# Powers in another tile, the finish over more heads, a later norm and an earlier start of sums in a two-block network

## The chip, the cores and the metric

The kernel runs on one core of a Trainium2 chip. The metric is the device time of one execution in microseconds; lower is better. Times come from the device, the rows from one execution that was taken with the hardware profiler.

## What is computed

Two blocks follow each other on one sequence of 1024 tokens with 1024 channels, in float32. The first block has two layers, each with a mixer and a feed-forward layer; the second block has an mLSTM branch, a state-space (S5) branch and gates.

```python
def first_block(x, ...):
    for layer in range(2):
        h = rmsnorm(x, mix_pre_g[layer])
        m = even_mixer(h, ...) if layer % 2 == 0 else odd_mixer(h, ...)
        x = x + rmsnorm(m, mix_post_g[layer])
        h = rmsnorm(x, ffn_pre_g[layer])
        x = x + rmsnorm(swiglu(h, w_gate, w_up, w_down), ffn_post_g[layer])
    return x

def second_block(h, ...):
    xn = rmsnorm_2(h, norm_pre_g)
    u_a, z_a, o_a, i_a, f_a, u_b, z_b, g_pre = split(xn @ w_in)
    y_a = mlstm_branch(u_a, z_a, o_a, i_a, f_a, ...) @ w_a_out
    y_b = s5_branch(u_b, z_b, lam_re, lam_im, log_dt, B, C, ...) @ w_b_out
    g = sigmoid(g_pre)
    return h + rmsnorm_2((g[..., :D] * y_a + g[..., D:] * y_b) @ w_o, norm_post_g)
```

The state-space branch needs, for each of its 16 groups of states, a table of 256 rotations exp(i n angle). It is built by doubling from the powers exp(i 2^k angle), k = 0 to 7.

## The kernel before, in words

**Tiles.** Activations lie with channels on the 128 partitions, as eight tiles of 128 channels by 512 tokens for each half of the sequence (half 0 and half 1). Every float32 product is made of three matmuls on a high and a low part of each operand. So each weight tile and each activation tile is first split: ScalarE writes the high part (L186 for weights, L246 for activations), VectorE or GpSimd subtracts it for the low part (L188, L248, L250).

**Buffers.** Tiles with one tag share a fixed number of buffers: 27 of tag `t4` (128 x 2 x 512), 18 of tag `t2` (128 x 512), one of `junk` (128 x 512 in bfloat16, 1024 bytes on a partition). Buffers are handed out when the program is built, in a planned order of the work. At run time an instruction that writes a buffer waits for the last readers of what was in it before. All loads and most stores are issued by SyncE's queue (SP) in that planned order, one behind the other.

**Side work.** Generators do work beside the main loop over matmuls. `start(g, rate)` enters one, each `tick` of the main loop advances it by `rate` steps, `drain(g)` runs what is left at once. The order in the program is the priority for the planner; each engine then executes its own list in order.

**First feed-forward layer, second product.** `ffn` multiplies in `ffn_down` (L632 to L634) by the down weights for half 0, then for half 1. Each takes 22 tiles of the hidden layer (`hid`, tag `t4`), which `hid_steps` loads from DRAM (`hidd`) into `t2` buffers called `xt` (L260) and splits (L246, L250). The 22 tiles of half 1 take the buffers of those of half 0. Beside the products of the first layer run `s5_tables` (rate 2.6): small operations of VectorE on tiles of 128 x 16, and from L1318 on GpSimd's loop over the pairs of groups. In each of its 8 rounds GpSimd builds two tables in the tile `s5R` with 48 multiplies, adds and subtracts and issues their two stores (L1335). The powers that it reads, `E`, are slices of the two `t2` tiles called `s5c`, which also hold the other constants and are stored to DRAM once (L1338).

**After it.** `finish_steps` for half 1 (the norm of the product, the sum with the residual, the statistics of the sum: 13 steps) runs beside the next mixer, `odd_mixer`, at one step a tick. That mixer goes over four heads for half 0, then for half 1; a head is `odd_conv` (PSUM tile `pxr`), `odd_gate` (`pg`) and `odd_rec` (`pr`, `pi`), two ticks each. At head 1, after its gate, `finished()` runs what is left of the finish, and `norm_steps` of half 1 starts: it makes the eight normed and split tiles `xs` that half 1's first `odd_conv` reads.

**Second block, late units.** `block2` ends its mLSTM branch beside five calls of `late_firsts`, each with two units of 24 matmuls (PSUM tile `pl`) on half 0's input, c = 28, 32, 36, 40, 44. Beside them `sum_steps` loads the kept input (`kept`) and makes from it the 19 sums and split tiles that `late_rest` reads next (20 steps, five for each of four groups of tiles).

Of the kernel before, what the change touches and what calls it, by code (L numbers as in the profile page):

```python
# [11 lines left out]
F32 = mybir.dt.float32  # L12
# [9 lines left out]
NT = 8  # L22
# [27 lines left out]
class Weights:  # L50
# [13 lines left out]
    def part(self, k0):  # L64
        return Weights(self.parts, self.q, self.k0 + k0)


class Model:
# [571 lines left out]
    def ffn(self, l, B, keep, pre, hook, beside, F, done=0):  # L640


        self.ahead = 90
        n = FFT // 2
        for j in range(n - F + done, n):
            if j == n - F + done + 3:
                self.finished()
                nb = self.start(self.ffn_sums(*pre, B, keep), 5.2 / (F - done - 3))
            self.ffn_first(l, 2 * j, B, None)
        self.drain(nb)  # L650
        self.ahead = 150
        hid = [], []
        for j in range(n):
            if j == n - 1:
                nb = self.start(self.hid_steps(0, hid[0]), 3.0)
            self.ffn_quad(l, 2 * j, B, j >= n - F)
        self.flush()
        self.drain(nb)
        self.ahead = 90
        bg = self.start(*beside)  # L660
        m, ss = self.ffn_down(l, 0, hid[0])
        hid[0].clear()
        nb = self.start(self.hid_steps(1, hid[1]), 3.0)
        self.drain(nb)
        self.finish(0, m, ss, "ffn_post_g", l)
        nb = self.start(chain(self.after(self.fin), hook()), 1.0)
        m, ss = self.ffn_down(l, 1, hid[1])
        self.drain(nb)
        self.drain(bg)
        self.finish(1, m, ss, "ffn_post_g", l)  # L670

    def after(self, g):

# [561 lines left out]
    def s5_tables(self):  # L1235
# [8 lines left out]
        def sm(n):  # L1244
            i = self.s5n[n] = len(self.s5n)
            return big[i // 32][:, i % 32]
# [31 lines left out]
        V.tensor_tensor(t0, mag, mag, ALU.mult)  # L1278
        V.tensor_tensor(self.rho4, t0, t0, ALU.mult)

        E = [(sm(f"er{k}"), sm(f"ei{k}")) for k in range(8)]
        cur = (cs, sn)
        for k in range(-2, 8):
            o = E[max(k, 0)]
            if k > -2:
# [32 lines left out]
        for g0 in range(0, 16, 2):  # L1318
            G.memset(R[:, :, 0, 0:1], 1.0)
            G.memset(R[:, :, 1, 0:1], 0.0)  # L1320
            for k in range(8):
                n = 1 << k
                er, ei = (E[k][i][:, g0:g0 + 2].unsqueeze(2).to_broadcast([128, 2, n]) for i in range(2))
                s, d = slice(0, n), slice(n, 2 * n)
# [526 lines left out]
    def block2(self, xsA, norm, dst):  # L1851

        io = self.io
        xs = [xsA, []]
        self.s5_in(xs[0], 0)
        self.xs_store(xs[0], 0)
        st = self.mconv(xs[0], 0, 0)
        g = self.start(self.mgates(xs[0], 0))
        self.mout(xs[0], 0, st)
        self.finished()  # L1860
        nb = self.start(norm(xs[1]), 3.0)
        self.mz(xs[0], 0, st)
        self.drain(nb)
        self.s5_in(xs[1], 1)
        self.xs_store(xs[1], 1)
        self.drain(g)
        self.start(self.s5_main(), 2.2)
        a = b = ()
        for h in range(NH):
            for hd in range(4):  # L1870
                units = 2 * ("o" not in st) + 2 * ("z" not in st) + 2 * (hd < 3 or h == 0) + 10 * (hd == 3 and h == 1)
                self.drain(a)
                a, b = b, self.start(self.mattn(h, hd, st), self.TH / units)
                new = None
                if "o" not in st:
                    self.mout(xs[h], hd, st)
                if hd < 3:
                    new = self.mconv(xs[h], h, hd + 1)
                if "z" not in st:
                    self.mz(xs[h], hd, st)  # L1880
                if hd == 3 and h == 0:
                    xs[1] = self.xs_load(1)
                    g = self.start(self.mgates(xs[1], 1))
                    new = self.mconv(xs[1], 1, 0)
                    self.drain(g)
                st = new

        x0 = self.xs_load(0)
        B = {"b11": x0[:4], "b21": x0[4:]}
        for c in range(28, 48, 4):  # L1890
            if c == 36:
                got = self.fetch([self.kept[h][k + j] for k in range(NT // 2) for j in (0, NT // 2) for h in range(2)])
                nb = self.start(self.sum_steps(lambda k, h: next(got), NT // 2, B), 1.75)
            self.late_firsts((c, c + 2), x0)
        self.drain()
        self.ahead = 150
        pre = [[], [], []], [[], [], []]
        for c in range(28, 48, 2):
            if c == 42:
                nb = self.start(self.merge_prep(1, *pre[1], 3), 1.6)  # L1900
            self.late_rest(c, B)
        self.drain(nb)
        self.ahead = 90
        nb = self.start(self.merge_prep(1, *pre[1]), 2)
        mg = self.merge(1, nb, *pre[1])
        nb = self.start(self.merge_prep(0, *pre[0]), 2.5)
        m, ss = self.proj_out(io["w2_o"], mg)
        self.drain(nb)
        self.finish(1, m, ss, "norm_post_g_2", 0, dst=dst(1))
        mg = self.merge(0, (), *pre[0])  # L1910
        m, ss = self.proj_out(io["w2_o"], mg, last=True)
        self.finished()
        self.finish(0, m, ss, "norm_post_g_2", 0, dst=dst(0), last=True)
        self.finished()

    def run(self, out):
        io = self.io
        xs = [None, None]
        part = lambda ap: lambda h: [ap[128 * k:128 * k + 128, h * T:h * T + T] for k in range(NT)]
        self.x, self.r = [part(io["x"])(h) for h in range(NH)], [None, None]  # L1920

        B, keep = [{}, {}], [[self.dp.tile([128, T], F32, name=f"keep{l}_{k}") for k in range(NT)] for l in range(2)]
        self.hidd = [[self.dp.tile([128, T], F32, name=f"hidd{h}_{j}") for j in range(FFT)] for h in range(NH)]
        self.kept = [[self.dp.tile([128, T], F32, name=f"kept{h}_{k}") for k in range(NT)] for h in range(NH)]
        self.lated = [{c: self.dp.tile([128, T], F32, name=f"lated{h}_{c}") for c in range(28, 48)} for h in range(NH)]
        self.m1l = {c: self.dp.tile([128, T], F32, name=f"m1l{c}") for c in range(28, 48, 2)}
        self.m1d = [self.dp.tile([128, T], F32, name=f"m1d{j}") for j in range(FFT)]

        def side():

            nb = self.start(self.norm_keep(0, "ffn_pre_g", 0, B[0], keep[0]))
            self.tick(1)
            self.drain(nb)
            self.ffn_first(0, FFT - 18, B[0], None)

        def hook(gname, gi, keep=None):
            def steps():
                xs[0] = []
                yield from self.norm_steps(0, gname, gi, xs[0], keep)
            return steps  # L1940

        self.ahead = 90
        self.layer0(lambda h, *m: self.finish(h, *m, "mix_post_g", 0, rate=1 + 0.25 * h, pool=h == 1), side)
        self.ffn(0, B[0], keep[0], ("ffn_pre_g", 0), hook("mix_pre_g", 1), (self.s5_tables(), 2.6), 9, 1)

        self.ahead = 90
        y, st = [[], []], {}
        for h in range(NH):
            for hd in range(4):
                if hd or not h:  # L1950
                    self.odd_conv(xs[h], h, hd, st)
                    self.odd_gate(xs[h], hd, st)
                if h == 0 and hd == 1:
                    self.finished()
                    xs[1] = []
                    nb = self.start(self.norm_steps(1, "mix_pre_g", 1, xs[1]))
                self.odd_rec(h, hd, st, y[h])
            if h == 0:
                self.drain(nb)
                st = {}  # L1960
                self.odd_conv(xs[1], 1, 0, st)
                self.odd_gate(xs[1], 0, st)
            else:
                self.finished()
                nb = self.start(self.norm_keep(0, "ffn_pre_g", 1, B[1], keep[1]), 1.2)
            self.finish(h, *self.proj_out(io["od_out"], y[h]), "mix_post_g", 1, rate=0.5 if h == 0 else 1.25, pool=h == 1)
        self.drain(nb)
        self.ahead = 90
        self.ffn(1, B[1], keep[1], ("ffn_pre_g", 1), hook("norm_pre_g_2", 0, self.kept[0]), (self.s5_tables2(), 2.6), 9)
        self.ahead = 90  # L1970
        self.block2(xs[0], lambda o: self.norm_steps(1, "norm_pre_g_2", 0, o, self.kept[1]), part(out))
# [66 lines left out]
```

## Time and profile before

| | us |
|---|---|
| median of three runs | 3279.76 (3275.04, 3279.76, 3284.11) |
| the profiled execution | 3275.86 |
| its span in the profile | 3274.2 |
| TensorE matmul busy | 3099.3 (95%) |
| VectorE busy | 2345.7 (72%) |
| ScalarE busy | 1532.8 (47%) |
| GpSimd busy | 803.9 (25%) |

Times in the rows are microseconds from the start of the span. PE is TensorE's matmuls, PEld its weight loads, DVE is VectorE, ACT ScalarE, POOL GpSimd, SPq SyncE's queue of DMA issues. A busy share tells only that an engine had an instruction running. Where an engine sat idle, the view of waits names what released it.

### The profile page before, as it was taken

To read this page: it belongs to the slowest core of one execution; us is meant where nothing else is said; L and a number is where in the kernel's file an instruction comes from. 1 tells how busy PE (TensorE), PEld (TensorE's weight loads), DVE (VectorE), ACT (ScalarE), POOL (GpSimd) and SP (SyncE) were. 2 spreads that over 40 slices of the span, in tenths; PEclk is the share of its full clock that TensorE was granted. 3 is DMA by queue.
4 is the path that set the end of the run, shared out by engine and by line. 5 is a ranking of instruction groups with operands and counts; after the bars stand their busy time and mean duration, and the time that the engine had idled before them with its cause. 6 is when DMAs were issued, how large, how long until landed. Compare 5 with 4: busy or idle time off the path is not lost. (4 is left out here: it accounts for less than half of the span.)

```text
span 3274.2 us, 42443 instructions
## 1 busy us (share of the span) xinstructions
PE 3099.3 (95%) x14200; PEld 2526.0 (77%) x14200; DVE 2345.7 (72%) x4489; ACT 1532.8 (47%) x2842; POOL 803.9 (25%) x1002
## 2 busy tenths in 40 slices
PE   8999999999994598999999999999999999999998
PEld 5777787888883487877888887777888778778886
DVE  8768857688862359777857888786688888765664
ACT  4646644333432237676443335544455444434442
POOL 4011102555367302111236540000111100153000
PEclk9999999999997799999999999999999999999999
DMA  4443445333532434334723345576644344745562
GB/s 156 157 143 127 145 153 191 103 126 126 191 115 103 151 121 150 101 125 162 253 93 130 126 144 191 199 226 240 214 136 154 129 153 136 257 140 196 187 209 97
DMA packets 227179, 511.84 MB, mean 156 GB/s; under 512 B 28040, under 2 KB 50760, under 8 KB 226960
## 3 DMA queue, kind: packets, MB, share of 16 engines
q1 hardware_dynamic: 225680, 504.93, 46.2%
q0 software_dynamic: 1280, 4.20, 0.3%
q8 instruction: 112, 1.84, 0.2%
q14 instruction: 107, 0.88, 0.1%
HBM read 386.21 MB, written 118.59 MB: 154 GB/s over the span
## 5 line engine op out<-in xcount | busy, mean ns | idle before, releaser
L188 DVE TENSOR_TENSOR wsp<-raw,wsp 128x512 fp32r<-128x512 f32 x850 | 629.8, 747 | 350.5 <-ACT wsp L186 347.2
L186 ACT ACTIVATE wsp<-raw 128x512 fp32r<-128x512 f32 x842 | 515.7, 616 | 722.5 <-PE pd L634 201.5
L632 PE MATMUL pd<-hid,wsp 128*128 128x512 f32 x704 | 279.2, 398 | 76.6 <-ACT hid L246 76.6
L633 PE MATMUL pd<-hid,wsp 128*128 128x512 f32 x704 | 278.9, 397 | 3.5 <-DVE hid L250 3.2
L634 PE MATMUL pd<-hid,wsp 128*128 128x512 f32 x704 | 277.6, 394 | 0.0
L632 PEld LDWEIGHTS pd<-hid,wsp 128*128 128x128 f32 x704 | 133.9, 190 | 105.6 <-ACT hid L246 78.7
L495 PE MATMUL qy<-st,wsp 128*128 128x512 f32 x464 | 180.7, 389 | 3.9 <-DVE st L248 3.9
L494 PE MATMUL qy<-st,wsp 128*128 128x512 f32 x464 | 181.1, 390 | 0.2 <-ACT st L246 0.2
L496 PE MATMUL qy<-st,wsp 128*128 128x512 f32 x464 | 180.6, 389 | 0.0
L526 POOL TENSOR_TENSOR qv<-qv,qu 128x512 f32<-128x512 f32 x54 | 90.6, 1677 | 341.8 <-ACT wsp L186 226.6
L633 PEld LDWEIGHTS pd<-hid,wsp 128*128 128x128 f32 x704 | 133.9, 190 | 37.3 <-DVE hid L250 10.1
L248 POOL TENSOR_TENSOR xs<-xt,xs 128x512 fp32r<-128x512 f32 x28 | 40.8, 1457 | 483.6 <-ACT xs L246 424.8
L634 PEld LDWEIGHTS pd<-hid,wsp 128*128 128x128 f32 x704 | 134.0, 190 | 26.9
L186 ACT ACTIVATE wsp<-wss 128x512 fp32r<-128x512 f32 x108 | 68.1, 631 | 183.9 <-PE qz L496 90.3
L494 PE MATMUL pf<-xs,wsp 128*128 128x512 f32 x288 | 114.0, 396 | 9.5 <-ACT m L572 8.5
L270 DVE TENSOR_TENSOR sq<-sq 128x512 f32<-128x512 f32 x140 | 99.0, 709 | 32.1 <-ACT sq L268 31.6
L250 DVE SCALAR_TENSOR_TENSOR hid<-xt,hid 128x512 fp32r<-128x512 f32 x88 | 58.0, 689 | 84.3 <-ACT hid L246 83.6
L495 PE MATMUL pf<-xs,wsp 128*128 128x512 f32 x288 | 113.3, 394 | 0.4 <-POOL xs L248 0.4
L496 PE MATMUL pf<-xs,wsp 128*128 128x512 f32 x288 | 113.3, 394 | 0.0
L405 POOL TENSOR_TENSOR xt<-xt,m 128x512 f32<-128x512 f32 x12 | 18.2, 1524 | 364.9 <-DVE m L402 356.7
L495 PEld LDWEIGHTS qy<-st,wsp 128*128 128x128 f32 x464 | 87.1, 188 | 22.1 <-DVE st L248 4.2
L494 PEld LDWEIGHTS qy<-st,wsp 128*128 128x128 f32 x464 | 87.1, 188 | 20.3 <-DVE qu L515 1.8
(720 smaller groups left out, 9106.3 us busy)
## 6 DMA issues: line engine op xcount, KB each, us to landing
raw<-in_w_in_dram SPq DMA_DIRECT2D x86, 512.0 KB
xt<-xres SPq DMA_DIRECT2D x128, 256.0 KB
raw<-in_wd_dram SPq DMA_DIRECT2D x64, 512.0 KB
raw<-in_wg_dram SPq DMA_DIRECT2D x62, 512.0 KB
raw<-in_wu_dram SPq DMA_DIRECT2D x62, 512.0 KB
hidd<-th SPq DMA_DIRECT2D x88, 256.0 KB
xt<-hidd SPq DMA_DIRECT2D x88, 256.0 KB
raw<-in_ev_in_dram SPq DMA_DIRECT2D x32, 512.0 KB
```

The costliest lines, as they stand in the source:

```text
L186: nc.scalar.activation(sp[:, 0], raw, AF.Copy)
L188: nc.vector.tensor_tensor(sp[:, 1], raw, f(sp[:, 0]), ALU.subtract)
L248: (low or nc.vector).tensor_tensor(t[:, 1], src, f(t[:, 0]), ALU.subtract)
L250: nc.vector.scalar_tensor_tensor(t[:, 1], src, scale, f(t[:, 0]), ALU.mult, ALU.subtract)
L270: nc.vector.tensor_tensor(q, q, acc, ALU.add)
L494: nc.tensor.matmul(ps, h, xs[k][:, 0], start=start and k == 0, stop=False, skip_group_check=not start)
L495: nc.tensor.matmul(ps, h, xs[k][:, 1], start=False, stop=False, skip_group_check=not start)
L496: nc.tensor.matmul(ps, l, xs[k][:, 0], start=False, stop=k == n - 1, skip_group_check=not start)
L526: nc.gpsimd.tensor_tensor(v5, v5, u3, ALU.add)
L632: nc.tensor.matmul(ps, h_, x[:, 0], start=k0 + k == 0, stop=False)
L633: nc.tensor.matmul(ps, h_, x[:, 1], start=False, stop=False)
L634: nc.tensor.matmul(ps, l_, x[:, 0], start=False, stop=k0 + k == FFT - 1)
```

## The change

There are four edits.

- In `s5_tables`, the 16 slices of `E` move from the `t2` tiles `s5c` to one tile of tag `junk`. That buffer belongs to the attention of the first layer (`attn`), which uses it as a scratch output; it has the same 1024 bytes on a partition. The names in `s5c` become 17 instead of 33, so they all lie in the first of its two tiles.
- The finish of half 1 after the first feed-forward layer gets 0.85 steps a tick instead of 1 (layer 1 keeps 1). The point where it has to be done moves from head 1 to head 2 of the mixer.
- With it, `norm_steps` of half 1 starts at head 2 and gets 1.2 steps a tick instead of 1. It still has to be done at the end of head 3.
- `sum_steps` of the kept input starts one call of `late_firsts` earlier (c = 32 instead of 36), with 1.3 steps a tick instead of 1.75.

```diff
@@ ffn
-        self.finish(1, m, ss, "ffn_post_g", l)
+        self.finish(1, m, ss, "ffn_post_g", l, rate=1 if l else 0.85)
@@ s5_tables
-        E = [(sm(f"er{k}"), sm(f"ei{k}")) for k in range(8)]
+
+        et = self._t([128, 16, 16], F32, "junk", 1, "s5e")
+        E = [(et[:, 2 * k], et[:, 2 * k + 1]) for k in range(8)]
@@ block2
-            if c == 36:
+            if c == 32:
...
-                nb = self.start(self.sum_steps(lambda k, h: next(got), NT // 2, B), 1.75)
+                nb = self.start(self.sum_steps(lambda k, h: next(got), NT // 2, B), 1.3)
@@ run
-                if h == 0 and hd == 1:
+                if h == 0 and hd == 2:
                     self.finished()
                     xs[1] = []
-                    nb = self.start(self.norm_steps(1, "mix_pre_g", 1, xs[1]))
+                    nb = self.start(self.norm_steps(1, "mix_pre_g", 1, xs[1]), 1.2)
```

## Rows read from the trace of the kernel before

**Rows 1.** The page's 40 slices (81.9 us each), busy tenths and granted clock

```profile
PE   8999999999994598999999999999999999999998
POOL 4011102555367302111236540000111100153000
PEclk9999999999997799999999999999999999999999
```

**Rows 2.** Waits, 1000 to 1110 us: waiting <- releaser, total, times, longest

```profile
ACT hid L246 <- DMA xt<-hidd: 75.5, 4, 73.1
...
PE pd L632 <- ACT hid L246: 72.2, 1, 72.2
```

**Rows 3.** Waits of SyncE's own queue, 980 to 1110 us

```profile
SPq L260 <- POOL s5rt L1330: 86.3, 1, 86.3
```

**Rows 4.** Instructions on tile s5c, 880 to 1110 us: durations ns, first and last start

```profile
L1330 POOL TENSOR_TENSOR s5rt<-s5R,s5c x64: 191/239/1063, 913.1 to 1096.1; 128x2 f32<-128x2 f32 x8, 128x4 f32<-128x4 f32 x8, 128x8 f32<-128x8 f32 x8, 128x16 f32<-128x16 f32 x8
...
L1295 DVE TENSOR_TENSOR s5c<-s5c x9: 167/169/266, 909.1 to 930.3; 128x16 f32<-128x16 f32 x9
...
L1338 SPq DMA_DIRECT2D s5c<-s5c x2: 326/326/327, 904.0 to 934.4; - x2
```

**Rows 5.** TensorE in order of time: its last before the idle piece, end of the product

```profile
1027.52 0.40 PE L634 MATMUL pd<-hid,wsp 128*128 128x512 f32 x1
...
1212.18 0.39 PE L632 MATMUL pd<-hid,wsp 128*128 128x512 f32 x1
...
1212.86 0.39 PE L236 MATMUL pxr<-xs,wsp 128*128 128x512 f32 x1
```

**Rows 6.** Stretches: length, busy us of each engine (instructions), clock, DMA share, GB/s

```profile
1008.80:1026.40 17.60, 15.24 (x52) 11.15 (x52) 13.02 (x29) 7.58 (x14) 11.53 (x32) 0.75 0.40 154
...
1099.90:1112.00 12.10, 11.92 (x38) 8.78 (x39) 6.99 (x11) 7.23 (x14) 0.00 (x0) 0.73 1.00 377
1112.00:1213.00 101.00, 101.00 (x454) 83.55 (x453) 55.49 (x92) 38.55 (x68) 5.85 (x4) 1.00 0.46 147
```

**Rows 7.** SyncE in order of time: the same 22 loads in layer 1

```profile
2105.45 15.24 SPq L260 DMA_DIRECT2D xt<-hidd  x22
```

**Rows 8.** ScalarE's splits of those 22 tiles, columns as in rows 4

```profile
L246 ACT ACTIVATE hid<-xt x22: 614/622/634, 2108.3 to 2125.8; 128x512 fp32r<-128x512 f32 x22
```

**Rows 9.** ScalarE in order of time: the first split of half 1's tiles

```profile
1005.85 0.62 ACT L246 ACTIVATE hid<-xt 128x512 fp32r<-128x512 f32 x1
```

**Rows 10.** Stretches of one GpSimd round each, columns as in rows 6

```profile
940.88:965.97 25.09, 25.09 (x112) 20.80 (x111) 8.83 (x13) 8.12 (x14) 18.14 (x53) 1.00 0.40 126
...
1060.90:1081.08 20.18, 0.00 (x0) 0.00 (x0) 0.00 (x0) 0.00 (x0) 15.12 (x52) 0.50 0.07 26
```

**Rows 11.** GpSimd in order of time after its last round

```profile
1097.84 1.13 POOL L1335 DMA_DIRECT2D s5r<-s5R  x2 [0.30 <-POOL s5R L1331]
1171.44 1.29 POOL L248 TENSOR_TENSOR xs<-xt,xs 128x512 fp32r<-128x512 f32 x1 [72.47 <-ACT xs L246]
1199.49 4.70 POOL L248 TENSOR_TENSOR xs<-xt,xs 128x512 fp32r<-128x512 f32 x3 [26.75 <-DVE wsp L188]
```

**Rows 12.** Longer stretches, heads 1 to 3 and the sums, columns as in rows 6

```profile
1240.00:1335.00 95.00, 86.35 (x368) 70.06 (x367) 90.45 (x151) 71.78 (x113) 23.50 (x16) 0.95 0.41 136
2797.00:2840.00 43.00, 43.00 (x219) 36.34 (x218) 23.29 (x48) 21.45 (x43) 3.22 (x6) 1.00 0.69 240
2840.00:2882.00 42.00, 31.77 (x129) 24.48 (x129) 39.53 (x52) 20.09 (x38) 23.99 (x15) 0.95 0.59 184
```

**Rows 13.** TensorE's longest wait, 1240 to 1335 us

```profile
PE pg L236 <- DVE l1h L727: 6.3, 1, 6.3
```

**Rows 14.** VectorE's groups of the norm steps, 1240 to 1335 us: busy, mean ns

```profile
L325 DVE SCALAR_TENSOR_TENSOR xt<-xt,pvt,rb 128x512 f32<-128x512 f32 x8 | 5.8, 739 | 1.1 <-PE rb L317 1.1
...
L248 DVE TENSOR_TENSOR xs<-xt,xs 128x512 fp32r<-128x512 f32 x4 | 3.8, 953 | 0.0
```

**Rows 15.** TensorE's longest wait, 2840 to 2890 us

```profile
PE qy L495 <- DVE st L248: 3.9, 1, 3.9
```

## The prediction, made before the changed kernel ran

> **What bounds the kernel now.** I read the page's slices first. TensorE is busy in 9 tenths or more of nearly every slice, so the kernel is bound by TensorE where nothing else stops it. Two neighbouring slices stand out with 4 and 5 tenths; there GpSimd is at 7 and 3 and the clock at 7 [rows 1]. The second view is that of the waits around these slices. TensorE sat idle for 72.2 us in one piece, waiting for ScalarE's split of a hidden tile, and ScalarE for the load of that tile [rows 2]. The third view is the wait of the queue that issues the load: SyncE stood 86.3 us on one issue of L260, released by GpSimd's L1330 [rows 3]. The fourth is the tile that this instruction reads: it is `s5c`. VectorE had written it for the last time at 930 us and SyncE had stored it at 934 us, but GpSimd read the powers in it until 1096 us [rows 4]. So a load of the second half's hidden tiles got the buffer of `s5c`, and waited until GpSimd's eighth round had read it. This one wait is what the first edit can reach. All other idle pieces of TensorE that I use below are under 7 us.
>
> **First edit: the powers in the tile `junk`.** Nothing is added or removed but the place of 16 slices; VectorE's and GpSimd's instructions stay. After it, the last accesses of `s5c` are VectorE's and the two stores', done some 70 us before the hidden loads are issued. The new tile's last reader is still GpSimd, but `junk` has no later user, and its earlier one, the first layer's attention, ended long before. So no load waits for GpSimd.
>
> The gain: half 1's product has 8 x 22 x 3 = 528 matmuls. At full clock three take 0.68 us (1212.18 to 1212.86), or 0.2267 us each [rows 5]. The wait of 72.2 us goes [rows 2]. So does what followed it: at the restart 38 matmuls took 12.1 us at a mean granted clock of 0.73, the lower level of 1.2 GHz at first after the idle time [rows 6]; at 0.2267 us they take 8.6 us, so 3.5 us come back. Together 75.7 us.
>
> What is late next? The other loads and splits of these 22 tiles. In layer 1 the same 22 loads were issued in 15.2 us [rows 7], and ScalarE's splits started 17.5 us apart, first to last [rows 8]. Here the first split started at 1005.85 us [rows 9], so the last is done near 1024 us. TensorE had used 15 tiles when it stopped at 1027.9 us [rows 5], and uses each in 3 x 0.2267 us, so this cover holds with some 4 us to spare; without it, the feed of one tile each 0.8 us instead of 0.68 costs at most 1 us. The losses at the start of the product, before 1026.4 us (15.2 us busy in 17.6 us, clock 0.75 [rows 6]), stay: the tiles wait there for half 0's buffers, as in layer 1.
>
> GpSimd itself is the next candidate, because its eight rounds don't get shorter, while TensorE arrives at the mixer 75.7 us sooner: at 1212.86 - 75.7 = 1137 us [rows 5]. A round takes 25.1 us when VectorE is busy for 8.8 us of it, and 20.2 us when VectorE is idle (18.1 against 15.1 us busy, the rest is a later landing of its own stores) [rows 10]. Before, three of the last four rounds ran while VectorE stood still. Now all four run against it: seven rounds of 25.1 us from 940.9 us end at 1117 us instead of 1099 us. GpSimd's next work, four of the eight splits of the mixer's input, comes at 1171 and 1199 us [rows 11], less 75.7 at 1096 and 1124 us. The first then waits about 21 us behind the tables, the others not at all, and TensorE wants them at 1137 us: 0 us, with 20 us of cover before it and about 7 us behind the tables for the other three. SyncE fetches three tiles ahead there, so the buffer that the first split holds longer stops no load.
>
> On this edit a rule speaks against the even pace of 25.1 us. The Trainium skill, page "SBUF — State Buffer", section "Who interferes with whom", says that a VectorE instruction with two SBUF inputs and a GpSimd instruction that reads SBUF exclude each other: who comes second stands for the whole instruction of the other. The rows agree in direction, 3.0 us more GpSimd time per round, but not with a full exclusion of each VectorE microsecond; what full exclusion would give is the first rival.
>
> **Second and third edit: the finish over more heads, the norm later.** No instruction is added. From 1240 to 1335 us TensorE is idle for 8.65 us, and the clock of 0.95 costs some 4 us more, while VectorE is busy for 90.45 of 95 us [rows 12]; the longest wait, 6.3 us, is for VectorE's convolution in head 2's gate [rows 13], among the norm steps. The finish (13 steps at 0.85: 15.3 of the 16 ticks before head 2's odd_rec) no longer ends in a burst at head 1, and the norm no longer falls on that gate. But VectorE's work in the stage stays the same, and the norm's eight steps now run in 6.7 ticks of the last eight: 5.8 + 3.8 = 9.6 us of VectorE time [rows 14], of which the last part is due just when half 1's first convolution wants `xs`. Bounds: a gain of 13 us if all of the loss goes, a loss of 10 us if the norm's work trails whole. Only 4.55 us of VectorE's idle time in the stretch can be put to use, so I take a gain of 2 us. No wait on a queue is added; the fetches of the norm are issued by SyncE about 25 us later, behind the same weight loads.
>
> **Fourth edit: the sums a call earlier.** Again nothing is added. The sums run while VectorE is full: from 2840 to 2882 us it is busy for 39.5 of 42 us, and TensorE idle for 10.2 us, with the clock at 0.95 (2 us more). In the 43 us before, VectorE is busy for only 23.3 us and TensorE never idle [rows 12]. In the full stretch TensorE's longest single wait, 3.9 us, is for VectorE's split of a sum [rows 15]. Starting one call earlier (48 matmuls, 10.9 us) moves sum work into the emptier stretch. Against it: the 19 split tiles and the 8 of the input fill all 27 `t4` buffers, so the splits can't start before the mLSTM branch has let its own go, and the 16 loads of `kept` now stand in SyncE's queue among that branch's. Bounds: a gain of 12 us, or a loss of 6 us, the size of the wait in [rows 13] where VectorE work was pushed in front of what TensorE needs. I take 4 us of gain, a third of the loss, since part of the start is held by the buffers.
>
> **Sum.** 75.7 + 2 + 4 = 81.7 us. The profiled execution took 3275.9 us (span 3274.2 and 1.7 around it), so 3194.2 us by it. It is among the faster ones: the median of the three is 3279.8, 3.9 us higher. I predict 3198 us. With both bounds of the small edits: 3279.8 - 75.7 - 13 - 12 = 3179 and 3279.8 - 75.7 + 10 + 6 = 3220.
>
> **Rivals.**
> *Full exclusion between VectorE and GpSimd.* From 1026.4 us GpSimd has 72.6 us of clean work left (its end at 1099.0 less 1026.4). VectorE's work in the stretch that moves up is 6.99 + 55.49 us in 113.1 us [rows 6], 0.55 of the time. If GpSimd stood in all of it, it would have done 50 us by 1137 us, and TensorE would wait some 23 us for the rest and about 3 us for the first splits: 3198 + 26 = 3224 us. Against it: 8.8 us of VectorE in a round cost 3.0 us [rows 10]. The Trainium skill's rule on that page, taken at its strictest, is this rival. Chance 0.05.
> *The load still waits.* Buffers are handed out again when the program is built; the load could get another one whose last access is GpSimd's or hangs on it, and the wait would only change its name. Then 3279.8 - 6 = 3274 us, within 0.3%. For it: the planner's order can't be read from the trace. Against it: in the rows GpSimd reads no `t2` tile in this stretch but `s5c` [rows 4]. Chance 0.07.
> *Slower: GpSimd's tables become the mixer's bound.* Place: GpSimd's queue, where the splits of `xs` stand behind the tables. Price: one microsecond for each by which GpSimd ends after 1137 us. It eats the whole gain if GpSimd ends after about 1219 us, 2.65 times its clean time from 1026.4 us; at 3 times, 1244 us, the kernel takes 3198 + 107 = 3305 us. Measured is 1.25 times [rows 10]. With the other tail cases, chance 0.03.
>
> **How the numbers follow.** The forecast, wait gone and the small edits within their bounds, has 0.85. The range runs from 3178 to 3222, its bounds; the rivals at 0.15 lie outside. A measurement can tell about 0.3%, 10 us, from no change. Faster by more: forecast and first rival, 0.90; within: 0.07; slower: 0.03.
>
> **What would show it.** In the changed kernel: SyncE's queue has no wait of L260 for GpSimd; the 22 loads go out in about 16 us; the two low slices of TensorE are at 9 but for some 10 us at the start of half 1's product; the mixer starts near 1137 us; GpSimd's last store is near 1117 us, after which its first split follows without a gap. Heads 1 to 3 keep most of their idle time, and the sums lose part of it. I am wrong if a wait of over 20 us remains in SyncE's queue between 1000 and 1110 us, if TensorE waits for GpSimd's `xs`, or if either small stage moves by over 13 us.

## The result and the profile after

The changed kernel takes 3193.03 us (median of four runs, 3189.33 to 3195.27) against 3279.6 us before: a ratio of 0.9735, 95% interval 0.9718 to 0.9752. Forecast were 3198 us in a range of 3178 to 3222. The profiled execution of the changed kernel took 3189.33 us, its span is 3187.6 us; the span is shorter by 86.6 us.

The slices of the page, for [rows 1]: busy tenths of TensorE and GpSimd and the granted clock, each slice 79.7 us.

```profile
PE   8999999999999999999999999999999999899998
POOL 4111002456447721112256620001010100252000
PEclk9999999999999999999999999999999999999999
```

The two low slices of TensorE are gone, and so is the drop of the clock. GpSimd has two slices of 7 beside a TensorE of 9: its tables now run beside TensorE's work.

SyncE's queue between 980 and 1110 us, the longest wait and two of the shorter ones, for [rows 3]; below it the same queue in order of time, to be set against [rows 7].

```profile
SPq L175 <- DVE wsp L188: 76.5, 19, 7.1
...
SPq L260 <- DMA xt<-hidd: 4.0, 13, 0.4
...
SPq L260 <- DVE hid L250: 0.4, 1, 0.4
```

```profile
1002.79 13.14 SPq L260 DMA_DIRECT2D xt<-hidd  x22
```

No wait for GpSimd is left there. The wait for `L188` is in 19 pieces, none over 7.1 us: weight loads that wait for a free buffer while three are loaded ahead. The 22 loads were out in 13 us. TensorE's two longest waits between 1000 and 1110 us, for [rows 2] (a third is of 0.2 us):

```profile
PE pd L633 <- DVE hid L250: 3.0, 1, 3.0
...
PE sst L281 <- DVE sq L270: 2.9, 1, 2.9
```

Both stand at the start of half 1's product, where they were before. TensorE in order of time at the end of the product, for [rows 5], and GpSimd's last tables and first splits, for [rows 11]:

```profile
1138.61 0.39 PE L634 MATMUL pd<-hid,wsp 128*128 128x512 f32 x1
1138.83 0.39 PE L236 MATMUL pxr<-xs,wsp 128*128 128x512 f32 x1
```

```profile
1129.30 1.14 POOL L1337 DMA_DIRECT2D s5r<-s5R  x2 [0.30 <-POOL s5R L1333]
1130.45 5.04 POOL L248 TENSOR_TENSOR xs<-xt,xs 128x512 fp32r<-128x512 f32 x4
```

The mixer begins at 1138.83 us instead of 1212.86 us. GpSimd's four splits are done at 1135.5 us, 3 us ahead of it.

Where the 86.6 us are: the first starts of TensorE's instructions on a tile (the view by tile gives them) cut the span into stages. The product stage goes from the first `pd` of the first layer to the first `pxr`, the mixer from there to its first `po`, the sums' stage from the first `pl` to the first `pgl`. The second half of the table has the experiments below.

| us | product | mixer, half 0 | first `pub` to first `pl` | sums | span | median |
|---|---|---|---|---|---|---|
| before | 330.1 | 148.4 | 551.0 | 222.3 | 3274.2 | 3279.6 |
| after | 254.4 | 144.8 | 548.6 | 217.8 | 3187.6 | 3193.0 |
| powers alone | 255.5 | 148.4 | 548.6 | 222.6 | 3198.1 | 3199.5 |
| all but the powers | 333.2 | 144.8 | 549.1 | 217.8 | 3268.8 | 3269.3 |
| powers, finish and norm | 255.7 | 144.6 | 549.4 | 222.4 | 3198.7 | 3200.0 |
| powers and sums | 253.4 | 146.9 | 548.6 | 217.5 | 3192.0 | 3195.4 |

Product -75.7, mixer -3.6, sums -4.5: 83.8 us. The other 2.8 us lie in stages that the edits don't touch, such as the mLSTM stage from `pub` to `pl`, where the executions shown differ by up to 2.4 us with no link to an edit.

### The profile page after: what moved, and what is told of

It reads as the page before. It is cut to its first block, busy times and chain, and to the rows that moved or that the text cites. A ratio compares the mean times of both kernels' runs of the same rounds, so it can differ in the third digit from the quotient of the medians.

```text
span 3187.6 us, 42447 instructions
## 1 busy us (share of the span) xinstructions
PE 3090.1 (97%) x14200; PEld 2521.7 (79%) x14200; DVE 2353.8 (74%) x4489; ACT 1531.7 (48%) x2842; POOL 827.8 (26%) x1002
## 5 line engine op out<-in xcount | busy, mean ns | idle before, releaser
L188 DVE TENSOR_TENSOR wsp<-raw,wsp 128x512 fp32r<-128x512 f32 x850 | 633.9, 752 | 333.7 <-ACT wsp L186 330.4
L270 DVE TENSOR_TENSOR sq<-sq 128x512 f32<-128x512 f32 x140 | 105.8, 757 | 30.8 <-ACT sq L268 30.4
L188 DVE TENSOR_TENSOR wsp<-wss,wsp 128x512 fp32r<-128x512 f32 x108 | 85.1, 789 | 22.3 <-ACT wsp L186 18.9
```

Source lines behind the costliest of these rows:

```text
L188: nc.vector.tensor_tensor(sp[:, 1], raw, f(sp[:, 0]), ALU.subtract)
L270: nc.vector.tensor_tensor(q, q, acc, ALU.add)
```

## The experiments

**The powers alone.** Of the four edits only this one:

```diff
-        E = [(sm(f"er{k}"), sm(f"ei{k}")) for k in range(8)]
+        et = self._t([128, 16, 16], F32, "junk", 1, "s5e")
+        E = [(et[:, 2 * k], et[:, 2 * k + 1]) for k in range(8)]
```

> Only the first edit (the powers in the tile junk). Theory A, the gain is the load that waited for GpSimd's last read of s5c: the mixer's first matmul comes about 75 us sooner than in the kernel before, the queue's wait for GpSimd is gone, and the time is 3279.6 - 75.7 = 3204 us. Rival B, the place of the powers matters little and the re-paced finish, norm and sums carry the gain: the time stays within 10 us of 3280 us.

Measured: 3199.5 us, ratio 0.9755 (0.9742 to 0.9769). The span went from 3274.2 to 3198.1 us, by 76.1 us, and the mixer begins at 1138.3 us, 74.6 us sooner. The product stage lost 74.6 us, and no L260 in SyncE's queue waits for GpSimd any more. So the first edit carries the gain, and its size by the profiled executions is the one of theory A. The medians are 80 us apart, 4 us more than that; the nine executions of before beside this run spread over 12 us (3274.2 to 3286.5).

**All but the powers.** The other three edits, with `E` left in `s5c`:

```diff
-        self.finish(1, m, ss, "ffn_post_g", l)
+        self.finish(1, m, ss, "ffn_post_g", l, rate=1 if l else 0.85)
...
-                if h == 0 and hd == 1:
+                if h == 0 and hd == 2:
...
-                    nb = self.start(self.norm_steps(1, "mix_pre_g", 1, xs[1]))
+                    nb = self.start(self.norm_steps(1, "mix_pre_g", 1, xs[1]), 1.2)
...
-            if c == 36:
+            if c == 32:
...
-                nb = self.start(self.sum_steps(lambda k, h: next(got), NT // 2, B), 1.75)
+                nb = self.start(self.sum_steps(lambda k, h: next(got), NT // 2, B), 1.3)
```

> The finish, norm and sums of the changed kernel, with the powers left in s5c. Theory A: the wait of over 70 us is still there; the time is about 3279.6 - 10 = 3270 us (between 3266 and 3276). Rival B: about 3200 us.

Measured: 3269.3 us, ratio 0.9966 (0.9953 to 0.9978). The wait is still there, in SyncE's queue and at TensorE (two views of waits, 980 to 1110 and 1000 to 1110 us):

```profile
SPq L260 <- POOL s5rt L1330: 86.7, 1, 86.7
```

```profile
PE pd L632 <- ACT hid L246: 73.9, 2, 73.1
```

The mixer and the sums have their shorter stages (144.8 and 217.8 us) with the wait in place: these parts don't lean on the first edit. Together the three edits take 10 us off the whole time here, and the interval lies below 1; so some gain of the small edits is shown, though not how it divides between them.

**The powers with the finish and the norm; the powers with the sums.** The first diff and the middle three, or the last two, pairs of lines of the second.

> The powers, the finish and the norm; the sums as before. The changed kernel's trace gives the mixer's stage some 5 us less than before, so theory A expects 3204 - 5 = 3199 us. Rival C, the 5 us of that stage come from elsewhere (the planner's order, the data of one execution): within 2 us of the run with the powers alone.

> The powers and the sums; finish and norm as before. From the first matmul of the late units to the first one behind the quads the changed kernel took 4.5 us less than before, and 2.4 us less in the mLSTM stage ahead of it. If both belong to the sums: 3204 - 7 = 3197 us. If only the first does: 3199.5 us. If neither does: 3204 us.

Measured: 3200.0 us (ratio 0.9752, 0.9739 to 0.9766) and 3195.4 us (0.9742, 0.9729 to 0.9756), on the chip on which the powers alone took 3199.5 us. With the sums the median is 4 us lower, the size that the forecast took, and the stage 5 us shorter; the single executions overlap a little (3193.8 to 3199.3 us against 3198.6 to 3203.5), so it is the stage that shows the gain. The 2.4 us of the mLSTM stage are not theirs, since the powers alone show them too. The finish and the norm shorten the mixer's stage: 144.6 to 144.8 us in the three kernels of the table that have them, 146.9 to 148.4 in the three that don't. (The expectation's 5 us for that stage was a misreading; by the table it is 3.6.) But the whole time with them is the same as without, which is what rival C said. In that execution the stretch from the first `po` to the first `pub` is 2.9 us longer than with the powers alone (884.0 against 881.1 us); in the changed kernel, which has the edit too, it takes 879.0, so this is not the edit's price. A stage of 2 to 4 us can be seen in a trace and still not be told from no change in the time of the kernel; whether the whole time gains by this edit stays open.

**Six rounds of tables in the kernel before.** GpSimd does six rounds, and the last four tables get copies of the first four, so the powers are read for a shorter time:

```diff
-        for g0 in range(0, 16, 2):
+        for g0 in range(0, 12, 2):
...
                 G.dma_start(self.s5r[g0 + i], R[:, i])
+                if g0 < 4:
+                    G.dma_start(self.s5r[g0 + 12 + i], R[:, i])
```

The tables of the last four groups are left out, so this time is not that of the full computation.

> The kernel before, with six of GpSimd's eight rounds; the last two pairs of tables are left out and get copies of the first two. If the load waits for GpSimd's last read of s5c, that read comes two rounds of 20 us sooner, less about 2 us for four more stores: some 38 us of the wait go, and the time is about 3241 us. If the wait were set by anything else (a store of s5c, VectorE, a DMA queue), it stays near 3280 us.

Measured: 3238.6 us, ratio 0.9876 (0.9860 to 0.9893). The waits of SyncE's queue and of TensorE, against 86.3 and 72.2 us before:

```profile
SPq L260 <- POOL s5rt L1330: 45.0, 1, 45.0
```

```profile
PE pd L632 <- ACT hid L246: 33.8, 1, 33.8
```

SyncE's wait is shorter by 41.3 us, TensorE's by 38.4 us, the kernel by 38.0 us (3276.6 us for the kernel before beside it). The same load waits for the same instruction, and moves with it. A store of `s5c` or VectorE, which were not touched, would not have moved it.

**Ten rounds in the changed kernel.** This tests the slower rival by its price. Two rounds are done twice:

```diff
-        for g0 in range(0, 16, 2):
+        for g0 in (0, 2, *range(0, 16, 2)):
```

> The changed kernel with ten rounds on GpSimd: the first two are done twice. In the changed kernel GpSimd ended its tables at 1130 us, its four splits at 1135.5 us, and TensorE began the mixer at 1138.8 us. Two rounds of 25 to 28 us more end at 1180 to 1187 us. If GpSimd's queue becomes the bound at one microsecond for one, as in the slower rival, TensorE waits for the splits until some 47 to 52 us after 1138.8 us, and the time is 3193 + 45 to 50 = 3238 to 3243 us. If the mixer has other cover, it stays near 3193 us.

Measured: 3232.3 us, ratio 0.9860 (0.9846 to 0.9875), 39.3 us over the changed kernel. TensorE's longest wait between 1130 and 1330 us, and GpSimd in order of time:

```profile
PE pxr L237 <- POOL xs L248: 37.1, 1, 37.1
```

```profile
1173.59 1.14 POOL L1337 DMA_DIRECT2D s5r<-s5R  x2 [0.30 <-POOL s5R L1333]
1174.74 4.95 POOL L248 TENSOR_TENSOR xs<-xt,xs 128x512 fp32r<-128x512 f32 x4
```

The mixer issued its first matmul at 1138.5 us and stood at the second, which reads the low part of the first split, until GpSimd had made it at 1176 us. So the place and the price of the rival are right: about one microsecond for each beyond the mixer's begin. The time is below what I expected because GpSimd ended at 1174.7 us, not 1180: once TensorE stands, VectorE has little to do, and GpSimd runs at its quick pace (its last round took 17.9 us, with VectorE idle all through it).

**Those four splits on VectorE**, in the changed kernel and with ten rounds:

```diff
-            out.append(self.split(t, "xs", low=nc.vector if k % 2 else nc.gpsimd))
+            out.append(self.split(t, "xs", low=nc.vector if k % 2 or (h, gname, gi) == (0, "mix_pre_g", 1) else nc.gpsimd))
```

> The changed kernel with the first mixer's four even splits of half 0 on VectorE instead of GpSimd. In the changed kernel GpSimd did them from 1130.5 to 1135.5 us, TensorE began the mixer at 1138.8 us: the cover held by 3 us. Theory A: nothing on the path, so within 3 us of 3193 us. If the splits behind the tables had cost something after all, it would be faster by that.

> The run with ten rounds of tables, with those four splits on VectorE. If the splits were the only place where the longer tables touched the path, the wait of 37 us at the mixer's first matmuls goes and the next user of GpSimd, the gelu of the first gate some 17 us into the mixer, becomes the place: TensorE then waits for a PSUM bank until GpSimd ends near 1180 us, 10 to 25 us, and the time is 3203 to 3218 us. If another thing than GpSimd's queue held TensorE, it stays near 3232 us.

Measured: 3195.0 us (ratio 0.9747, 0.9733 to 0.9760) and 3209.9 us (0.9796, 0.9782 to 0.9809). The first says that the changed kernel loses nothing to GpSimd's queue, though its cover is 3 us thin. The second: of the 39 us that ten rounds cost, 22 go when the splits leave GpSimd, and the rest moves on to the next user of that queue (three lines of the view of waits, 1130 to 1250 us, with TensorE's longest, and GpSimd after its tables):

```profile
ACT gl L737 <- DVE gl L736: 19.4, 1, 19.4
DVE gl L736 <- POOL gl L735: 19.2, 1, 19.2
...
PE pi L236 <- ACT ra L772: 14.1, 1, 14.1
```

```profile
1175.86 1.13 POOL L1337 DMA_DIRECT2D s5r<-s5R  x2 [0.30 <-POOL s5R L1333]
1177.07 0.62 POOL L735 TENSOR_SCALAR gl<-gl 128x512 f32<-128x512 f32 x1
```

L735 is the first gate's gelu; in the changed kernel it ran at 1156 us. The view names each step but one: VectorE's L736 waited for GpSimd's L735, ScalarE's L737 for VectorE's L736, and TensorE for ScalarE's L772. That L772 was late because it stands behind L737 I read from ScalarE's list in order of time (L737 at 1178.45 us, L772 at 1180.50).

**The sums over ten units.** Started at c = 28 with 1.05 steps a tick:

```diff
-            if c == 32:
+            if c == 28:
...
-                nb = self.start(self.sum_steps(lambda k, h: next(got), NT // 2, B), 1.3)
+                nb = self.start(self.sum_steps(lambda k, h: next(got), NT // 2, B), 1.05)
```

> The changed kernel with the sums started at the first late call (c = 28) at 1.05 steps a tick. If VectorE's idle time is what the earlier start uses, there is still some ahead of it: 1 to 4 us faster than 3193 us. If the t4 buffers that the mLSTM branch holds set the start of the splits: no change, or slower by the loads that stand in SyncE's queue.

Measured: 3195.9 us, ratio 0.9747 (0.9733 to 0.9762), as the changed kernel: the gain of 1 to 4 us did not come. The two stretches of the late units that answer to [rows 12], 3.7 us and 46.7 us behind the first `pl`: this run, then the changed kernel.

```profile
2724.30:2767.30 43.00, 38.29 (x186) 31.70 (x185) 26.82 (x47) 23.02 (x44) 5.24 (x7) 0.96 0.65 232
2767.30:2809.30 42.00, 39.14 (x177) 31.86 (x177) 37.20 (x54) 20.68 (x39) 20.90 (x14) 1.00 0.58 198
```

```profile
2714.90:2757.90 43.00, 42.69 (x216) 35.98 (x215) 29.63 (x55) 23.68 (x47) 5.87 (x7) 1.00 0.76 269
2757.90:2799.90 42.00, 33.48 (x139) 26.72 (x138) 37.29 (x47) 18.15 (x34) 21.49 (x14) 0.92 0.48 166
```

In the full stretch TensorE's idle time falls from 8.5 to 2.9 us, but 4.7 us of it come up in the stretch ahead of it, where VectorE is far from full. TensorE's waits there (2724.3 to 2767.3 us):

```profile
PE pl L494 <- DVE lt L1766: 3.0, 1, 3.0
PE s5py L1491 <- DMA s5OK<-s5k: 1.3, 1, 1.3
PE mpx L1668 <- DVE mdm L1677: 0.5, 1, 0.5
```

The longest is for VectorE's L1766, which works on the result of a late unit, so VectorE is late in places though it is not full. Whether the `t4` buffers play a part, as the second expectation has it, was not tried.

## Why the prediction was right, point by point

- **The bound.** That one load waited for GpSimd's last read of `s5c`: shown. The wait goes when the powers move, stays when all else moves, and follows GpSimd's end when rounds are taken away. One reading of [rows 4] was off, without effect: VectorE's last write of `s5c` is that of L1313 at 934.2 us, not of L1295 at 930, still 162 us before GpSimd's last read. By the order of the names all 16 slices of `E` lay in the first of the two tiles, not in both.
- **75.7 us for the first edit.** The product stage is shorter by 75.7 us in the changed kernel and by 74.6 us with the powers alone. Both terms, the 72.2 us of idle time and the 3.5 us of the lower clock after it, are gone: from 1019.7 to 1083.3 us TensorE has no idle time and the granted clock is 1.00 (the rows of rounds below).
- **What is late next, the loads and splits.** The 22 loads were out in 13.1 us (15.2 in layer 1), and TensorE waited 3.0 us at the start of the product and not after it. The loss at the start stayed, as forecast. But the splits were slower than forecast. They start 24.8 us apart, first to last, not 17.5, and the last ends at 1032.5 us, not near 1024:

```profile
L246 ACT ACTIVATE hid<-xt x22: 614/617/632, 1007.1 to 1031.9; 128x512 fp32r<-128x512 f32 x22
```

  ScalarE has splits of weights between them in its list, and stood 8.4 us before one of these. No matmul of the product waited for a split of a hidden tile after the start, so this cost nothing. That TensorE had used 15 tiles when it stopped is not in [rows 5]; ScalarE had split 15 by then.
- **What is late next, GpSimd.** The result was right, the term was mis-sized. Forecast were rounds of 25.1 us and an end at 1117 us; the end is 1130.4 us. Of the 20 us of cover between the tables and the mixer 8 are left. The other three splits, forecast to come 7 us behind the tables, stood behind them as well; all four were done 3 us before the mixer. The 25.1 us were read from a round with 8.8 us of VectorE work [rows 10], but the stage that moves up has more. Four rounds of the changed kernel, columns as in [rows 6]:

```profile
967.43:992.91 25.48, 25.48 (x114) 21.09 (x113) 8.17 (x13) 7.91 (x14) 18.16 (x53) 1.00 0.39 114
...
1019.69:1052.54 32.85, 32.85 (x145) 26.08 (x144) 28.59 (x43) 19.99 (x37) 26.58 (x53) 1.00 0.62 213
1052.54:1083.31 30.77, 30.77 (x138) 25.47 (x137) 16.43 (x25) 11.76 (x21) 23.43 (x52) 1.00 0.60 185
1083.31:1108.17 24.86, 24.66 (x115) 20.31 (x114) 14.45 (x29) 7.23 (x14) 19.14 (x52) 1.00 0.53 174
```

  The fifth round stands beside the splits of the hidden tiles and 28.6 us of VectorE, and takes 32.9 us. I had the 0.55 of VectorE's time in that stretch at hand for the first rival and didn't use it for the forecast.
- **Full exclusion, the first rival.** It did not come. Against a round without VectorE (15.1 us of GpSimd [rows 10]), GpSimd's busy time grows by 3.0, 11.5, 8.3 and 4.0 us with 8.2, 28.6, 16.4 and 14.5 us of VectorE: 0.3 to 0.5 us for each. The rule of the Trainium skill, page "SBUF — State Buffer", section "Who interferes with whom", has the right sign here; a full microsecond for each would be the double or more. A single operation of GpSimd does stand while one of VectorE's runs, as the last section shows; what did not come is that VectorE's whole busy time is lost to GpSimd.
- **The load still waits, the second rival.** It did not come: no L260 in SyncE's queue waits for GpSimd.
- **The slower rival.** Its mechanism is there, as ten rounds show; eight rounds end 8 us before the mixer begins, and the four splits behind them 3 us before it.
- **Finish and norm, 2 us.** The stage gained 3.6 us, within the bounds of -10 and 13. The longest wait in it went from 6.3 us [rows 13] to 4.0 us and stands where it stood, at head 2's gate, so taking the norm off that gate did not free it:

```profile
1216.80 0.47 PE L236 MATMUL pg<-xs,wsp 128*128 128x512 f32 x1 [4.03 <-DVE l1h L727]
```

  In the whole time nothing is seen.
- **The sums, 4 us.** The stage gained 4.5 us. The loss in the full stretch fell from 10.2 to 8.5 us of idle time [rows 12]. The wait for the split of a sum, 3.9 us [rows 15], is gone there, as meant; with the powers alone it is still 3.1 us. Most of it came back in the wait for the factor of a norm, in the kernel before (2840 to 2882 us) and the changed one (2757.9 to 2799.9 us):

```profile
PE rb L317 <- DVE nr L310: 1.5, 1, 1.5
```

```profile
PE rb L317 <- DVE nr L310: 4.9, 1, 4.9
```

  What makes up the rest of the 4.5 us stays open.
- **The base.** I added 3.9 us, since the profiled execution of before was that far below its median. The changed kernel's stands 3.7 us below its own, so the step held. By profiled executions 3194.2 us were forecast and 3189.3 measured; 2.8 of the 4.9 us lie in stages that the edits don't touch.

## What to carry to other kernels

When all engines stop at once, go from the wait of the engine to the wait of the queue that issues its load, and from there to the last reader of the buffer: the tile that is held too long may belong to work that has nothing to do with the stage. A few small values that a slow engine reads for long should not share a buffer with anything that others are waiting to reuse. And where side work on another engine stays as long as it was while the main path gets shorter, price its pace from the work that will stand beside it, not from a quiet stretch.

## What the runs showed of the hardware

GpSimd's pace hangs on VectorE more than I had assumed: the same 48 small operations with their two stores took 20.2 us a round beside an idle VectorE and 32.9 us beside one that was busy for 28.6 us. That it is VectorE, and not ScalarE, TensorE or the transfers that also run then, the single operations show. Here is one shape of GpSimd's operation twice in the changed kernel, then two of VectorE's:

```profile
1052.72 3.57 POOL L1328 TENSOR_TENSOR s5rt<-s5R,s5e 128x2 f32<-128x2 f32 x1
...
1108.36 0.19 POOL L1328 TENSOR_TENSOR s5rt<-s5R,s5e 128x2 f32<-128x2 f32 x1
```

```profile
1055.57 0.68 DVE L405 TENSOR_TENSOR xt<-xt,m 128x512 f32<-128x512 f32 x1
1056.47 0.69 DVE L405 TENSOR_TENSOR xt<-xt,m 128x512 f32<-128x512 f32 x1 [0.23 <-DMA xt<-xres]
```

The long one began while VectorE ran six two-input operations without a gap (1052.56 to 1056.25 us), and ended at 1056.29 us, in VectorE's first pause. The short one began just before an operation of VectorE (1108.41 us). Set against the same operations of a quiet round (from 1061.0 us in the kernel before), the changed kernel's 384 take 39.9 us more; 39.5 of these lie in the 202 that overlap an instruction of VectorE. The other 182 take some 2 ns more each, also the 79 of them beside ScalarE. Twelve that overlapped only VectorE's L325 or L402, whose second tensor comes from PSUM, took 6 ns more each.

It also feeds back: with ten rounds, as soon as TensorE stood and VectorE with it, GpSimd sped up, and the tables ended 5 to 12 us before what an even pace gives.
